# Running column sums on VectorE and loads on GpSimd's queue in a 2-D prefix-sum kernel

## The chip, the cores and the metric

The kernel runs on one core of a Trainium2 chip. The metric is the device time of one execution in microseconds (us). Every time below is the median of runs of one kernel, all fast. A ratio is the mean time of one kernel's fast runs over that of the other kernel's fast runs of the same rounds, so it is not quite the ratio of the medians quoted beside it. The "span" of a profile is some 2 us shorter than the device time, because it starts with the first instruction.

## The reference

Four matrices of 4224 x 4224 fp32 numbers (285.5 MB in all) are summed in two dimensions; the diagonal of the result is then summed once more.

```python
def reference(x):                      # x: (4, 4224, 4224) fp32
    ps = np.cumsum(np.cumsum(x, axis=1), axis=2)
    diag = np.diagonal(ps, axis1=1, axis2=2)
    return np.cumsum(diag, axis=1).astype(np.float32)
```

The diagonal element ps[i,i] is the sum of the upper left square. It grows from i-1 to i by the part of row i up to the diagonal and the part of column i above it. So the kernel needs, for every i, one row sum (to the left) and one column sum (above), and each element of the input is read once. What is left is a short chain of prefix sums.

## The kernel before

It walks through each image in 11 strips of 384 rows. A strip holds three rows in each of 128 partitions (P = 128, F = 3, GW = 384, NG = 11), and three strip buffers are in use. Strip g needs row sums over the columns left of the diagonal block, masked sums in the block itself, and column sums over all columns from the block on. This is the part that the change replaces (cuts marked):

```python
def load_rows(o, b, r0):
    nc.sync.dma_start(out=o, in_=x[b, r0 : r0 + GW, :].rearrange("(p f) w -> p f w", f=F))
# ...
def act_sum(acc, src):                              # row sum on ScalarE, output thrown away
    dump = dumpool.tile([P, 2688], BF16, name="dump")
    nc.scalar.activation(out=dump[:, :w], in_=src, func=ACT.Copy, accum_out=acc)
# ...
def add_up(strip, g, ws):
    k = row_of(g)
    hi = (g + 1) * GW
    mu = mup.tile([P, F, GW], FP32, name="mu")
    for q in range(F):
        act_sum(acc[:, k, q, 0:1], strip[:, q, :ws])             # ScalarE: 5/8 of the columns
    for q in range(F):
        block = strip[:, q, g * GW : hi]
        masked(mu[:, q, :], block, um3[:, q, :], ...)            # VectorE: diagonal block into mu
    for q in range(1, F):
        add_to(mu[:, 0, :], mu[:, q, :])
    columns(g, mu[:, 0, :], minus_sel)                           # TensorE: block's columns
    if hi < N:
        for q in range(1, F):
            add_to(strip[:, 0, hi:], strip[:, q, hi:])           # VectorE: 3 rows to 1
        for j in range(g + 1, NG):
            columns(j, strip[:, 0, j * GW : (j + 1) * GW])       # TensorE: all other columns
    for q in range(F):
        pair_sum(acc[:, k, q, 1:2], strip[:, q, ws:hi])          # VectorE: the other 3/8
```

At the end of the last image, strip 9 comes (strips count from 0), then the last 384 rows in pieces ("part_a", "part_b"). A chain of small steps closes the sum: row sums into PSUM, two scans (`c`), the rows' weights (`arows`, `fin_a`, `fin_b`, `fin_e`), and two small output transfers.

## Time and profile before

| | before |
|---|---|
| time, first runs | 677.53 us (676.79 to 678.20) |
| transfer queue busy | 98.2% of the span |
| VectorE, TensorE, ScalarE busy | 57%, 42%, 29% |
| last strip lands, end of span | 655.6 us, 675.7 us |

The table reads as follows: no engine is near its limit, and the input stream is nearly always at work. The trace holds sixteen completion records for each input transfer. I take them for one of each of the core's 16 DMA engines; the records carry no engine's name, so that a late record comes from the same engine every time is inferred from its steady delay. A transfer counts as landed when the sixteenth is there. I read these records one by one, and I call "lag" the distance from their median to the last of them.

### The profile page before, as it was taken

The numbers are of one execution on the slowest core, as the hardware profiler recorded it, in microseconds if no ns is written. First come the engines' busy times: TensorE is split into PE (matmuls) and PEld (weight loads), VectorE is DVE, ScalarE is ACT, GpSimd is POOL, SyncE is SP. The second block draws the span as 40 slices with busy tenths as digits, with TensorE's granted clock in tenths as the row PEclk, the third lists the DMA queues.
The fourth block names the chain that finished last, engine by engine and source line by source line (L and its number), as shares of the span: only waits on it lengthen the run. The fifth ranks groups of instructions, "written<-read, shape, count | busy, mean of one in ns | idle before, by whom it ended". The sixth has DMA issues, their size and how long they took to land.

```text
span 675.7 us, 2520 instructions
## 1 busy us (share of the span) xinstructions
PE 281.8 (42%) x576; PEld 70.3 (10%) x576; DVE 387.9 (57%) x738; ACT 198.0 (29%) x275; POOL 7.1 (1%) x30
## 2 busy tenths in 40 slices
PE   0366455521037644532105545543212555663224
PEld 0021111100002111100001111100000111110002
DVE  1678666443377766444347776544445777554556
ACT  0121322334412122233451112223453111222446
POOL 4000000000000000000000000000000000000000
PEclk9977766665557777755556877775655687766666
DMA  9999999999999999999999999999999999999993
GB/s 384 432 419 433 432 432 433 438 439 430 432 432 432 435 436 432 433 432 432 432 435 432 432 433 431 432 432 432 432 432 436 432 432 433 432 432 430 435 400 128
DMA packets 7938, 285.69 MB, mean 423 GB/s; under 512 B 840, under 2 KB 1396, under 8 KB 2164
## 3 DMA queue, kind: packets, MB, share of 16 engines
q1 hardware_dynamic: 7924, 285.55, 98.2%
q8 instruction: 4, 0.07, 0.0%
q14 instruction: 10, 0.08, 0.0%
HBM read 285.47 MB, written 0.07 MB: 423 GB/s over the span
## 4 chain that ended last, share of the span: by engine, by line
DMA 72%; DVE 13%; PE 11%; ACT 2%; issue 1%; SPq 0%; DVEq 0%; ACTq 0%
DMA strip<-in_x_dram 72%; PE d L207 10%; DVE strip L236 8%; DVE mu L239 2%; ACT dump L214 2%; DVE mu L236 2%; PE fin_b L207 0%; DVE pair L225 0%; DVE c L377 0%; PE fin_a L207 0%; SPq L69 0%; DVE c L239 0%; DVE pu L219 0%; DVE yl L416 0%; DVE r L219 0%
## 5 line engine op out<-in xcount | busy, mean ns | idle before, releaser
L214 ACT ACTIVATE dump<-strip 128x224 bf16<-128x224 f32 (+13 forms) x137 | 184.0, 1343 | 453.4 <-DMA strip<-in_x_dram 450.4
L207 PE MATMUL d<-strip,sel 128*33 128x384 f32 (+1 forms) x440 | 223.3, 677 | 130.6 <-DVE strip L236 130.6
L239 DVE SCALAR_TENSOR_TENSOR mu<-strip,um 128x384 f32<-128x384 f32 x129 | 65.2, 555 | 265.0 <-DMA strip<-in_x_dram 265.0
L236 DVE TENSOR_TENSOR strip<-strip 128x3840 f32<-128x3840 f32 (+9 forms) x80 | 188.4, 2355 | 1.4
L207 PE MATMUL d<-mu,minus_sel 128*33 128x384 f32 (+1 forms) x86 | 51.9, 698 | 249.6 <-DVE mu L236 249.6
L207 PEld LDWEIGHTS d<-strip,sel 128*33 128x33 f32 (+1 forms) x440 | 58.2, 140 | 301.6 <-DVE strip L236 170.5
L225 DVE SCALAR_TENSOR_TENSOR pair<-strip 128x80 bf16<-128x80 f32 (+12 forms) x138 | 81.7, 592 | 3.2
L236 DVE TENSOR_TENSOR mu<-mu 128x384 f32<-128x384 f32 x86 | 47.8, 556 | 1.5
L207 PEld LDWEIGHTS d<-mu,minus_sel 128*33 128x33 f32 (+1 forms) x86 | 7.2, 122 | 283.9 <-DVE mu L236 280.9
L214 ACT ACTIVATION_READ_ACCUMULATOR dump<-strip 128x1 f32 x137 | 25.5, 186 | 0.0
L225 DVE DVE_READ_ACCUMULATOR pair<-strip 128x1 f32 x138 | 11.3, 82 | 0.0
L239 DVE DVE_READ_ACCUMULATOR mu<-strip,um 128x1 f32 x129 | 10.7, 83 | 0.0
L214 ACT ACT_TABLE_LOAD x1 | 1.3, 1283 | 19.1 <-DMA strip<-in_x_dram 19.1
L207 PE MATMUL d<-ones_all,r 128*33 128x128 f32 (+1 forms) x12 | 2.3, 346 | 5.9 <-DVE r L219 5.9
L200 DVE TENSOR_SCALAR steps<-steps 128x128 int32<-128x128 int32 x1 | 0.5, 461 | 5.8 <-POOL steps L199 5.8
L207 PE MATMUL fin_a<-weights,arows 128*1 128x256 f32 (+1 forms) x4 | 1.4, 513 | 3.1 <-DVE arows L219 3.1
L207 PEld LDWEIGHTS d<-ones_all,r 128*33 128x33 f32 (+1 forms) x12 | 1.4, 132 | 8.7 <-issue 5.3
L219 DVE TENSOR_REDUCE r<-acc 128x99 f32<-128x297 f32 (+1 forms) x2 | 0.7, 360 | 2.6 <-ACT dump L214 2.6
L207 PE MATMUL fin_b<-weights,bsum 128*1 128x128 f32 (+2 forms) x12 | 2.1, 364 | 0.0
L377 DVE TENSOR_TENSOR_SCAN c<-ones_all,carry,c 33x384 f32<-33x384 f32 (+1 forms) x2 | 2.0, 1008 | 0.1
L102 DVE MEMSET um<- 128x1152 bf16 (+1 forms) x2 | 1.4, 698 | 1.1 <-PEq L465 1.1
L377 DVE TENSOR_TENSOR_SCAN c<-ones_all,carry,d 33x384 f32<-33x384 f32 (+1 forms) x2 | 2.0, 1002 | 0.1
(62 smaller groups left out, 23.8 us busy)
## 6 DMA issues: line engine op xcount, KB each, us to landing
strip<-in_x_dram SPq DMA_DIRECT2D x43, 6336.0 KB, 32.1
strip<-in_x_dram SPq DMA_DIRECT2D x1, 2304.0 KB
strip<-in_x_dram SPq DMA_DIRECT2D x1, 1536.0 KB
strip<-in_x_dram SPq DMA_DIRECT2D x3, 480.0 KB, 31.4
head<-in_x_dram SPq DMA_DIRECT2D x1, 576.0 KB
strip<-in_x_dram SPq DMA_DIRECT2D x1, 352.0 KB, 32.0
strip<-in_x_dram SPq DMA_DIRECT2D x1, 128.0 KB, 24.7
out_dram<-c SPq DMA_DIRECT2D x1, 49.5 KB
```

The lines of the kernel that those rows point to most:

```text
L102: nc.vector.memset(um, -1.0)
L200: nc.vector.tensor_single_scalar(out=steps, in_=steps, scalar=2, op=ALU.arith_shift_right)
L207: nc.tensor.matmul(o, lhsT=lhsT, rhs=rhs, start=start, stop=False, skip_group_check=True)
L214: nc.scalar.activation(out=dump[:, :w], in_=src, func=ACT.Copy, accum_out=acc)
L219: nc.vector.reduce_sum(out=acc, in_=src, axis=AX.X)
L225: nc.vector.scalar_tensor_tensor(out=pair[:, :w], in0=src[:, :w], scalar=1.0, in1=src[:, w:], op0=ALU.mult, op1=ALU.add, accum_out=acc,)
L236: nc.vector.tensor_add(out=o, in0=o, in1=i)
L239: nc.vector.scalar_tensor_tensor(out=o, in0=i, scalar=1.0, in1=m, op0=ALU.mult, op1=ALU.mult, accum_out=acc,)
L377: nc.vector.tensor_tensor_scan(out=c12[:, i, :], data0=ones_row[:rows], data1=src, initial=carry[:, i : i + 1], op0=ALU.mult, op1=ALU.add,)
```

## The change

The intent is to take work off TensorE: columns above the diagonal are added up on VectorE into one running row `u` per partition, and TensorE reads only 384 columns of it per strip. Masks are turned from -1 to 1. ScalarE now sums all the columns of a row and writes its unused output over the strip. The masked block is written over the strip too. All strips load by GpSimd's queue, and strip 9 of the last image comes in three transfers, one per row q ("thirds" below). Smaller edits are left out here, such as the place of the first sum of part_a, which now comes later. In diffs `...` and comment lines stand for code that is cut.

```diff
+    load = nc.gpsimd.dma_start
     def act_sum(acc, src):
-        dump = dumpool.tile([P, 2688], BF16, name="dump")
-        nc.scalar.activation(out=dump[:, :w], in_=src, func=ACT.Copy, accum_out=acc)
+        nc.scalar.activation(out=src, in_=src, func=ACT.Copy, accum_out=acc)
 ...
-        def add_up(strip, g, ws):            # shown above
+            for q in range(F):
+                act_sum(rsum[:, k, q : q + 1], strip[:, q, :hi])
+            block = strip[:, :, lo:hi]
+            nc.vector.tensor_mul(out=block, in0=block, in1=um3)
+            row_sums(rabove[:, k, :], block)
+            if g == 0:
+                nc.vector.tensor_add(out=u, in0=strip[:, 0, :], in1=strip[:, 1, :])
+                add_to(u, strip[:, 2, :])
+            else:
+                for q in range(F):
+                    add_to(u[:, lo:], strip[:, q, lo:])
+            columns(g, u_of(g))
 ...
+        if not whole:                        # strip 9 of the last image
+            columns(LG, head[:, 0, :])
+            for q in range(F):
+                load(out=strip[:, q, :], in_=rows_of(b, g)[:, q, :])
+            for q in range(F):
+                act_sum(rsum[:, k, q : q + 1], strip[:, q, :wa])
+                pair_sum(more[:, q : q + 1], strip[:, q, wa:hi])
+                masked(block, block, um3[:, q, :], rabove[:, k, q : q + 1])
+                add_to(u[:, lo:], strip[:, q, lo:])
+            for j in (g, LG):
+                columns(j, u_of(j))
```

## The prediction

> **What bounds the kernel now.** I read the page first: the head, the busy line of each engine, the slices, the queues.
>
> ```profile
> span 675.7 us, 2520 instructions
> ...
> PE 281.8 (42%) x576; PEld 70.3 (10%) x576; DVE 387.9 (57%) x738; ACT 198.0 (29%) x275; POOL 7.1 (1%) x30
> ...
> GB/s 384 432 419 433 432 432 433 438 439 430 432 432 432 435 436 432 433 432 432 432 435 432 432 433 431 432 432 432 432 432 436 432 432 433 432 432 430 435 400 128
> ...
> q1 hardware_dynamic: 7924, 285.55, 98.2%
> q8 instruction: 4, 0.07, 0.0%
> q14 instruction: 10, 0.08, 0.0%
> ```
>
> No compute engine is over 57% busy, while the one transfer queue is busy for 98.2% of the span and the rate stands at 432 to 433 GB/s in nearly every slice. 285.5 MB at 432 GB/s are 661 us. The kernel is a stream of input; compute matters only in the last 20 us, or if a buffer came free too late. So I then read how early transfers are asked for (the list of transfer issues), and the windows of the end:
>
> ```profile
> strip<-in_x_dram SPq DMA_DIRECT2D x43, 6336.0 KB, 32.1
> ```
>
> ```profile
> 500.00:640.00 140.00, 64.63 (x134) 14.14 (x134) 84.44 (x149) 36.00 (x54) 0.00 (x0) 0.67 1.00 433
> ...
> 660.00:665.00 5.00, 1.90 (x8) 0.48 (x6) 4.22 (x14) 4.91 (x7) 0.00 (x0) 0.84 0.79 310
> 665.00:670.00 5.00, 1.80 (x10) 0.62 (x11) 4.08 (x12) 4.81 (x13) 0.00 (x0) 0.50 0.07 27
> 670.00:676.00 6.00, 3.48 (x24) 2.38 (x22) 1.91 (x9) 0.47 (x2) 0.00 (x0) 0.50 0.00 0
> ```
>
> A strip (6.49 MB) takes 15.0 us to stream, and is issued 32.1 us before it lands: 45 - 32 = 13 us after the landing of the strip whose buffer it takes, with two others queued. There is slack of some 15 us. In the windows the last two columns are the DMA share and GB/s: from 665 on only 7% of the engines' capacity moves anything. I wanted to know why it is not zero, and why the last strip's compute starts at 655.68:
>
> ```profile
> 620.77 34.83 DMA strip<-in_x_dram
> 655.68 2.31 ACT dump L214 x2
> 658.00 2.31 ACT dump L214 x2
> 660.33 0.93 ACT dump L214
> ...
> 665.52 1.01 DVE c L377
> 666.56 1.00 DVE c L377
> 667.56 0.47 DVE pair L225 x2
> ```
>
> The trace keeps a completion record of each of the 16 DMA engines for each transfer. For the last strip 15 of them are at 649.10 to 651.04 us, and the sixteenth at 655.60. In the first strip the same gap is small (15 within 17.83 to 18.48, the last 19.06). So **one of the sixteen engines falls behind** during the run, and every strip waits for it. The packet records say why: its 50,688-byte packets, 1.875 us as a median, take 2.25 to 2.53 us at 55, 105, 145, 161, 254, 282, 403, 419, 421, 509, 564 and 615 us, and beside each of these there is a packet of an instruction queue (q14: 8,192 bytes; q8: 16,384 bytes). Instructions are fetched over that engine. In the strips' time 9 x 8,192 + 4 x 16,384 bytes went there, which at its 27.0 GB/s is 5.1 us; its lag against the median engine grew from 1.0 to 5.7 us, by 4.7. The end is the slow engine's landing (655.6) plus 20.1 us of chain; its very last piece lands at 669.96, and 5.8 us follow.
>
> **What the Trainium skill says.** (1) "DMA: Bandwidth & Descriptors", Where 436 GB/s comes from: the ports allow 435.2 GB/s. The trace agrees: 432 to 433. So no way of issuing can gain more than 0.7% of rate. (2) The same page, Latency and other measured facts, says that engines 7 and 15 are usually slower and puts this, as a guess, to the descriptor rings of the GpSimd (software) path, with no size. The trace before has no software queue, so it can't show it; its own straggler has the other cause above. (3) "SBUF — State Buffer", Who interferes with whom: VectorE in a 2-port mode locks GpSimd out and so starves its descriptor writing; `tensor_tensor` and `tensor_reduce` were not seen to. All large VectorE work after the change is of those two kinds; no run here shows it yet. (4) "VectorE: DVE Perf Modes", The TRN2 errata, gives (N+151)/0.96 ns for an fp32 add: 4.157 us for 3,840 columns. The trace agrees, 4155 ns:
>
> ```profile
> L236 DVE TENSOR_TENSOR strip<-strip 128x3840 f32<-128x3840 f32 x8 | 33.2, 4155 | 0.1
> ```
>
> **The change part by part.**
> TensorE: before, strip g sends 1 + (10-g) products of 384 columns, six on average; after, one. From 440 + 86 passes to about 90, at 0.68 to 0.70 us: 275 us of busy time become about 62, none of it on the path except in the tail.
> VectorE: the three masked blocks, two adds per block and pair sums (65.2 + 47.8 + 81.7 us) go, bar the tail. One multiply and one reduction of 1,152 elements come, 1.36 us by the add's formula and 1.35 (the head's reduction took 1347 ns). Adds into the running row: three per strip instead of two, over 384 more columns: three of 4.155 us for g=1 down to three of 0.94 for g=10, with two of 4.56 us for g=0. An image is 80 us of adds and 30 us of multiply and reduction, about 110; three of them, 100 for the nine first strips of the last and some 28 for the rest: **VectorE about 457 us**, from 388. Still under the 661.
> ScalarE: all columns up to hi instead of 5/8 of them. From 2400 columns in 2203 ns and 224 in 390: 0.203 us + 0.833 ns a column, + 0.19 for the accumulator. An image: 77 us; in all about 300, from 198.
> Buffer release: ScalarE now writes the strip in place, so VectorE must wait for all three sums, then works. g=1: 3 x 1.03 + 2.7 + 3 x 4.155 = 18.3 us after landing; g=5: 6.9 + 2.7 + 7.7 = 17.3; g=10: 11.7 + 2.7 + 2.8 = 17.2. Before it was 13. The other two strips last until 30 us after landing, so 12 us of slack remain less the GpSimd's time to write descriptors (a few us at most, my choice). VectorE's largest strip, 15.2 us, equals the stream's period only once per image, so no backlog builds. I take the stream to stay full.
> Queue: the bytes are the same, and packets should keep their 50,688 bytes. I choose the same rate, give or take 1%. The small head goes first by the old queue and should cover the new queue's start.
> Instructions: VectorE falls from 738 to about 285, TensorE and its loads from 1152 to about 260; GpSimd gains some 50. 2520 become about 1250. Half the fetches mean half the lag of the straggler: **-2.5 us**.
> Tail: the last strip comes in three pieces, so that at its landing L only one third is left: ScalarE 2.3 us, VectorE 2.5 (pair 0.9, mask 0.6, add 0.95), two products (1.5), the row sums into PSUM (0.9), the old sequence to the second scan (4.9), pair sums, row sum, closing products and output as before (8.2): L + 18.5 where it is L + 20.1 now. The last piece lands at L + 14.4 and needs at least some 4 us, also L + 18.4. Saving **1.6 us**, no more, as both limits meet there.
> Sum: 677.5 - 2.5 - 1.6 = 673.4, and I put 0.6 us on for a slower software queue: 674.0.
>
> **The rivals.**
> (A) The software queue is slower: ring reads, an engine that lags, or smaller packets. For: the skill's note on engines 7 and 15. Against: nothing in the trace. At 425 GB/s instead of 432 it is +11 us, 685; at 415, over 690.
> (B) Late buffers: descriptor writing is held up while VectorE runs (68% of the time), or the serial ScalarE-VectorE path eats the slack. It would show as slices below 430 GB/s. Against: 12 us of slack. It would be 680 to 700.
> (C) VectorE becomes the bound: 457 us against 661 speaks against it; only g=1 touches 15 us.
> (D) All hidden: the straggler stays (descriptors in place of instructions) and the tail is tied to the last landing: 676 to 678.
> (E) A gain over 2% (below 664.2): 661 us of stream plus 2 us of start alone come to 663, so the tail would have to vanish. Nearly excluded.
>
> **Range and chances.** My centre is 674.0. Without the straggler at all and with the tail's gain it would be about 670, a little better rate 667; (A) in a mild form gives 684. So 667 to 684 for 8 in 10. Over 691 needs (A) or (B) in earnest: 9%. Faster by over 2%: 2%. Within: 89%.
>
> **What would show it.** The queue's line must read software instead of hardware at the same MB, with 432 GB/s in the slices; TensorE below 90 us, VectorE 440 to 470, ScalarE near 300; fewer instruction packets, and the sixteenth landing of the last strips 2 to 4 us behind the rest rather than 5 to 6. From the last strip's landing to the end it should be 18 to 19 us. The prediction is wrong if slices drop below 425 GB/s, if packets are split, or if the gap between a landing and the next issue exceeds 27 us.

## The result, and the profile after

The changed kernel took 678.24 us (677.90 to 679.04, four runs) beside 677.75 us of the kernel before. The ratio is 1.0011, with a 95% interval of 0.9993 to 1.0028. A gain of 3.5 us was forecast; none came.

The first lines of the changed kernel's page, its slices and its queues:

```profile
span 676.2 us, 1095 instructions
...
PE 73.6 (11%) x138; PEld 12.8 (2%) x138; DVE 449.0 (66%) x277; ACT 276.3 (41%) x275; POOL 35.0 (5%) x81
...
GB/s 371 432 435 435 432 435 435 435 441 435 438 435 432 435 432 432 432 432 432 432 432 432 432 432 432 432 435 432 432 432 432 435 432 432 432 432 430 416 418 101
...
q0 software_dynamic: 7392, 284.89, 97.7%
q1 hardware_dynamic: 468, 0.66, 0.3%
q14 instruction: 7, 0.06, 0.0%
q8 instruction: 1, 0.02, 0.0%
```

The reader sees a large change that did what it was meant to do. TensorE fell from 281.8 to 73.6 us, instructions from 2520 to 1095, instruction packets from 14 to 8, and the stream kept its 432 GB/s on the new queue, but for 416 and 418 in the two slices from 625 to 659 us (the kernel before has 435 and 400 there, and e3_after_syncq below, on the old queue, 420 and 417). The stream even ended sooner. These are the completion records of both kernels (us; my reading of the traces):

```
                                 before: median  last   lag     after: median  last   lag
strip 8 of the last image             634.91  640.54   5.63         634.33  636.43   2.10
strip 9 (after: its last third)       649.90  655.60   5.69         649.49  651.61   2.12
last piece of all                     664.10  669.77   5.67         663.72  665.81   2.09
```

The last strip landed 4.0 us sooner, and so did the last piece. The end of the span did not move: from the landing of strip 9 to the end it was 20.1 us (675.7 - 655.6) and is now 24.6 us (676.2 - 651.6). The tail took back what the stream gave. The chain of waits of the changed kernel shows where (start, length, what):

```profile
608.94 27.49 DMA strip<-in_x_dram
...
636.54 5.00 ACT strip L211 x3
...
642.59 3.26 ACT strip L211 x3
...
645.88 1.37 DVE strip L297
...
649.92 1.37 DVE u L231
...
659.12 0.97 DVE u L231
...
660.14 3.64 PE d L205 x10
```

In the kernel before, the chain waits for strip 9. Here the last transfer in it is strip 8, which landed at 636.4 us. From then on it is work, 40 us of it: ScalarE until 645.8, VectorE until 660.1. VectorE's own timeline has the reason in its first line, in brackets (idle time before, and what ended it):

```profile
645.88 1.36 DVE L297 TENSOR_TENSOR strip<-strip,um 128x1152 f32<-128x1152 f32 x1 [7.97 <-ACT strip L211]
...
652.59 0.95 DVE L220 SCALAR_TENSOR_TENSOR pair<-strip 128x768 f32<-128x768 f32 x1
...
659.12 0.96 DVE L231 TENSOR_TENSOR u<-u,strip 128x768 f32<-128x768 f32 x1
```

VectorE stood idle for 8 us with strip 8 in memory, because ScalarE's three sums of 3,456 columns had to end first (9.2 us). It then did strip 8 (6.7 us) and the thirds of strip 9 one after another (7.4 us). Two of these thirds had landed long before. When the last third landed at 651.6, VectorE was 8.5 us away from the end of its work on it. In the kernel before, nothing wrote the strip that ScalarE was reading except past its columns, and VectorE started on strip 9 with the landing:

```profile
655.69 0.56 DVE L239 SCALAR_TENSOR_TENSOR mu<-strip,um 128x384 f32<-128x384 f32 x1 [8.08 <-DMA strip<-in_x_dram]
```

The same wait is there in nearly all strips. It is the longest line of VectorE in the list of waits (us in total, times, longest):

```profile
DVE strip L297 <- ACT strip L211: 203.4, 39, 10.4
```

These 203 us cost nothing in the earlier strips, since the stream does not wait for them: transfers were still issued 27.9 us (median) before they landed; e6_last_only below tests it.

### The profile page after: what moved, and what is told of

The parts are those of the page before. It is cut to its first block, busy times and chain, and to the rows that moved or that the text cites. A ratio compares the mean times of both kernels' runs of the same rounds, so it can differ in the third digit from the quotient of the medians.

```text
span 676.2 us, 1095 instructions
## 1 busy us (share of the span) xinstructions
PE 73.6 (11%) x138; PEld 12.8 (2%) x138; DVE 449.0 (66%) x277; ACT 276.3 (41%) x275; POOL 35.0 (5%) x81
## 4 chain that ended last, share of the span: by engine, by line
DMA 73%; ACT 10%; DVE 9%; issue 6%; PE 2%; ACTq 0%; DVEq 0%; POOLq 0%
DMA strip<-in_x_dram 73%; ACT strip L211 10%; DVE u L231 4%; DVE u L300 1%; DVE strip L297 1%; DVE above L214 1%; PE d L205 1%; DVE pair L220 1%; DVE c L379 0%; PE fin_b L205 0%; DVE strip L234 0%; PE fin_a L205 0%; DVE pu L214 0%; DVE c L234 0%; ACTq L211 0%
## 5 line engine op out<-in xcount | busy, mean ns | idle before, releaser
L211 ACT ACTIVATE strip<-strip 128x768 f32<-128x768 f32 (+11 forms) x137 | 270.5, 1975 | 389.0 <-DMA strip<-in_x_dram 374.7
L231 DVE TENSOR_TENSOR u<-u,strip 128x3840 f32<-128x3840 f32 (+10 forms) x121 | 299.1, 2472 | 2.9
L297 DVE TENSOR_TENSOR strip<-strip,um 128x1152 f32<-128x1152 f32 x42 | 57.0, 1357 | 203.4 <-ACT strip L211 203.4
L205 PE MATMUL d<-u,sel 128*33 128x384 f32 (+1 forms) x88 | 65.0, 844 | 593.9 <-DVE u L231 593.9
L214 DVE TENSOR_REDUCE above<-strip 128x3 f32<-128x1152 f32 x42 | 56.8, 1353 | 1.5
L292 POOL DMA_DIRECT2D strip<-in_x_dram x39 | 20.7, 530 | 574.6 <-DVE u L231 535.8
L211 ACT ACTIVATION_READ_ACCUMULATOR strip<-strip 128x1 f32 x137 | 25.5, 186 | 0.0
L205 PEld LDWEIGHTS d<-u,sel 128*33 128x33 f32 (+1 forms) x88 | 7.6, 134 | 648.7 <-DVE u L231 647.7
L300 DVE TENSOR_TENSOR u<-strip 128x4224 f32<-128x4224 f32 x4 | 18.2, 4549 | 0.0
L220 DVE SCALAR_TENSOR_TENSOR pair<-strip 128x384 f32<-128x384 f32 (+5 forms) x12 | 6.9, 577 | 0.2
L352 POOL DMA_DIRECT2D strip<-in_x_dram x5 | 2.7, 552 | 4.7 <-DMA strip<-in_x_dram 4.7
L316 POOL DMA_DIRECT2D strip<-in_x_dram x3 | 1.6, 528 | 14.2 <-issue 14.2
L341 POOL DMA_DIRECT2D strip<-in_x_dram x2 | 1.4, 709 | 13.2 <-issue 13.2
L86 POOL DMA_DIRECT2D strip<-in_x_dram x3 | 1.7, 594 | 0.8 <-POOLq L467 0.8
## 6 DMA issues: line engine op xcount, KB each, us to landing
strip<-in_x_dram POOLq DMA_DIRECT2D x42, 6336.0 KB, 27.9
```

The costliest lines, as they stand in the source:

```text
L86: load(out=t, in_=rows_of(0, i))
L205: nc.tensor.matmul(o, lhsT=lhsT, rhs=rhs, start=start, stop=False, skip_group_check=True)
L211: nc.scalar.activation(out=src, in_=src, func=ACT.Copy, accum_out=acc)
L214: nc.vector.reduce_sum(out=acc, in_=src, axis=AX.X)
L220: nc.vector.scalar_tensor_tensor(out=pair[:, :w], in0=src[:, :w], scalar=1.0, in1=src[:, w:], op0=ALU.mult, op1=ALU.add, accum_out=acc,)
L231: nc.vector.tensor_add(out=o, in0=o, in1=i)
```

## The experiments

**Theory.** Two things moved in opposite directions. (1) The DMA engine that lags is held up by instruction fetches; the change halved them, so landings came 4 us sooner. (2) In the last strips VectorE waits for ScalarE, since both write over the strip, and this costs the end some 5 us. **Rivals.** For the stream: the new queue removed the lag. For the tail: the closing products at a lower clock, or the last landing and what must follow it, set the end anyway.

All of the following runs were correct, with five rounds each beside the kernel before; e7_best has four timed runs and the changed kernel four. By a margin of 2% every one of them counts as "same", so the differences below are small ones, told by their intervals.

| run | median us | ratio to before | 95% interval | span us |
|---|---|---|---|---|
| changed kernel | 678.24 | 1.0011 | 0.9993 to 1.0028 | 676.2 |
| e1_scratch | 678.43 | 1.0008 | 0.9995 to 1.0022 | 676.8 |
| e2_apart | 673.17 | 0.9932 | 0.9920 to 0.9945 | 671.3 |
| e3_after_syncq | 678.14 | 1.0001 | 0.9988 to 1.0013 | 676.4 |
| e4_before_poolq | 677.65 | 0.9994 | 0.9981 to 1.0006 | 675.8 |
| e5_pad | 678.33 | 1.0010 | 0.9998 to 1.0023 | 676.6 |
| e6_last_only | 673.17 | 0.9927 | 0.9914 to 0.9941 | 671.5 |
| e7_best | 671.81 | 0.9914 | 0.9900 to 0.9927 | 669.8 |
| e8_pad_dve | 681.50 | 1.0061 | 1.0047 to 1.0075 | 679.3 |
| e9_pad_late | 681.15 | 1.0051 | 1.0037 to 1.0065 | 679.8 |

### The tail: who writes the strip

**e1_scratch** takes away one of the two writes:

```diff
-        nc.scalar.activation(out=src, in_=src, func=ACT.Copy, accum_out=acc)
+        dump = dumpool.tile([P, N], BF16, name="dump")
+        nc.scalar.activation(out=dump[:, : src.shape[-1]], in_=src, func=ACT.Copy, accum_out=acc)
```

> The changed kernel, with ScalarE's sums written to a bf16 scratch row instead of over the strip; the masking of the diagonal block still writes the strip in place. Theory (the tail's delay is that VectorE must wait for all three ScalarE sums of strip 8 of the last image): the masked block still overwrites columns that ScalarE has to read first, so this half of the undoing alone changes nothing: VectorE starts on that strip at about 645.9 us as in the changed kernel, end near 676 us, ratio to before 1.000. Rival (ScalarE's write into the strip is the whole of the wait): VectorE starts at the landing, 636.5 us, and the kernel ends near 670.5 us, ratio 0.990.

VectorE's first line on strip 8 in this run:

```profile
646.09 1.36 DVE L300 TENSOR_TENSOR strip<-strip,um 128x1152 f32<-128x1152 f32 x1 [7.96 <-ACT dump L212]
```

Nothing changed: the same idle time, the same engine named, and the same time of the kernel. ScalarE's write is not needed for the wait. VectorE's masked block overwrites columns that ScalarE has yet to read, and that alone keeps it waiting.

**e2_apart** takes the second write away as well:

```diff
-            nc.vector.tensor_mul(out=block, in0=block, in1=um3)
-            row_sums(rabove[:, k, :], block)
-            # adds over u[:, lo:] from the strip
+            nc.vector.tensor_mul(out=mu, in0=block, in1=um3)
+            row_sums(rabove[:, k, :], mu)
+            # adds over u[:, lo:hi] from mu, over u[:, hi:] from the strip
```

> As the run before, and the masked block goes to a tile of its own, so that nothing writes a strip any more and VectorE need not wait for ScalarE at all. Theory: VectorE starts on strip 8 of the last image at its landing (636.5 instead of 645.9 us), is through the last third of strip 9 at 654 instead of 660 us, and the span becomes 670 to 671 us, ratio to before 0.990 to 0.992. Rival (the tail is set by something else, the closing products at a lower clock or the last landing): VectorE starts early, but the end stays at 675 to 676 us, ratio 0.998 to 1.001.

VectorE in this run, on strip 8 and on the last add of strip 9:

```profile
637.38 1.36 DVE L301 TENSOR_TENSOR mu<-strip,um 128x1152 f32<-128x1152 f32 x1 [6.56 <-DMA strip<-in_x_dram]
...
654.14 0.96 DVE L234 TENSOR_TENSOR u<-u,strip 128x768 f32<-128x768 f32 x1
```

VectorE starts with the landing (this run's strip 8 landed at 637.35), and what ends its idle time is now the transfer. The last add is 5.0 us sooner, and the span is 4.9 us shorter, although strip 8 landed 0.9 us later than in the changed kernel. From the last third's landing (652.51) to the end it is now 18.8 us instead of 24.6. The time is 0.8% below the changed kernel's by the two ratios. The gain that the stream had made is now visible in the time.

The rival of the lower clock falls as well. In the changed kernel the granted clock was 0.50 while the four passes on `u` ran (660.14 to 662.87 us), and in e7_best below it was 1.00; the passes took 2.73 us in both. The profiled run of e1_scratch had a clock of 1.00 throughout and the changed kernel's time.

**e6_last_only** asks where the wait counts: the two tiles of their own are used in strip 8 of the last image alone.

```diff
+            apart = not whole and g == LG - 2
             for q in range(F):
-                act_sum(rsum[:, k, q : q + 1], strip[:, q, :hi])
+                act_sum(rsum[:, k, q : q + 1], strip[:, q, :hi], dump[:, :hi] if apart else None)
-            nc.vector.tensor_mul(out=block, in0=block, in1=um3)
+            masked_block = mu if apart else block
+            nc.vector.tensor_mul(out=masked_block, in0=block, in1=um3)
```

> The changed kernel with the separate tiles for ScalarE's output and the masked block in one strip alone, strip 8 of the last image. Theory (only the wait in that strip reaches the end; in the 41 others it lies under the transfers): at least as fast as with all strips apart, span 670 to 671.5 us, ratio 0.991 to 0.993. Rival (the waits in the earlier strips held transfers up too): half or less of the gain, ratio 0.996 or more.

One strip of 42 gives the whole gain: 0.9927 beside 0.9932. VectorE here goes from strip 7's work straight on to strip 8, 1.4 us after its landing (637.11), and in this run's list of waits it still waits for ScalarE in 38 strips:

```profile
638.50 1.35 DVE L307 TENSOR_TENSOR mu<-strip,um 128x1152 f32<-128x1152 f32 x1
...
DVE strip L307 <- ACT strip L211: 196.0, 38, 10.4
```

Taking these waits away as well (e2_apart) gained nothing more.

**e7_best** goes on from there. In strip 9 the running row is finished first, and its products start before the pair sums:

```diff
-                pair_sum(more[:, q : q + 1], strip[:, q, wa:hi])
-                masked(block, block, um3[:, q, :], rabove[:, k, q : q + 1])
-                add_to(u[:, lo:], strip[:, q, lo:])
-            for j in (g, LG):
-                columns(j, u_of(j))
+                masked(mu[:, q, :], block, um3[:, q, :], rabove[:, k, q : q + 1])
+                add_to(u[:, hi:], strip[:, q, hi:])
+                add_to(u[:, lo:hi], mu[:, q, :])
+                if q == F - 1:
+                    for j in (LG, g):
+                        columns(j, u_of(j))
+                pair_sum(more[:, q : q + 1], strip[:, q, wa:hi])
```

> As the run before, and in the last strip the running row is finished first (mask, add the columns above, add the block) and its products start before the pair sums. From the last strip's landing to the row sums in PSUM it should be 5 us where it was 6.4. Theory (the chain from that landing sets the end): about 1 us less than the run before, ratio 0.990 to 0.992. Rival (the last landing, near 666 us, and what must follow it set the end by now): less than 0.4 us better than the run before.

TensorE's timeline in this run has both groups of products:

```profile
652.51 2.73 PE L205 MATMUL d<-u,sel 128*11 128x384 f32 x4 [7.71 <-DVE u L233]
655.03 1.49 PE L205 MATMUL d<-ones_all,r 128*11 128x128 f32 x6
```

They start 1.1 us after the landing (651.39) and are done 5.1 us after it. The median is 1.4 us below e6_last_only, but the intervals of the two ratios overlap. The profiled runs differ in their lag too (2.1 us at the last piece here, 2.6 in e6_last_only), and the last third landed 0.9 us sooner. From that landing to the end it was 19.2 us in e6_last_only and is 18.4 here, so in these two runs 0.8 us is the reordering and the rest came with the stream. This version beats the kernel before by 0.9% and the changed kernel by 1.0%. From its last landing (665.93) to its end it is 3.9 us, of which the output transfers at the end are over 2, so little is left in the tail.

### The stream: what holds one engine back

**e3_after_syncq** is the changed kernel on the old queue, **e4_before_poolq** the kernel before on the new one:

```diff
 # e3_after_syncq
-    load = nc.gpsimd.dma_start
+    load = nc.sync.dma_start
 # e4_before_poolq, all loads but the head
-        nc.sync.dma_start(out=o, in_=x[b, r0 : r0 + GW, :] ...
+        nc.gpsimd.dma_start(out=o, in_=x[b, r0 : r0 + GW, :] ...
```

> The changed kernel with its strips loaded by the old queue of SyncE; nothing else. Theory (the slowest DMA engine lags because instructions are fetched over it, and there are fewer of them now): the lag of the sixteenth landing behind the median stays near 2 us at the end, the last landing near 666 us, time as in the changed kernel within 1 us, ratio 1.000 to 1.002. Rival (the queue removed the lag): the lag is 5 to 6 us as in the kernel before, last landing near 670 us, and the time 3 to 4 us longer, ratio 1.005 or more. A third (the queue costs something that hides a gain): ratio below 0.998.

> The kernel before with all its loads but the head issued by GpSimd's queue; its instructions otherwise as they were. Theory (instruction fetches make the lag): the lag stays 5 to 6 us, last landing near 670 us, ratio 0.999 to 1.003. Rival (the queue makes or removes the lag): the lag falls to about 2 us and the time by 3 to 4 us, ratio near 0.995.

Span and strip queue of e3_after_syncq, then of e4_before_poolq:

```profile
span 676.4 us, 1096 instructions
...
q1 hardware_dynamic: 8212, 285.55, 98.0%
```

```profile
span 675.8 us, 2520 instructions
...
q0 software_dynamic: 7104, 284.89, 97.8%
```

The four combinations of kernel and queue, lag at the last piece (us): before on the old queue 5.67, before on the new one 5.40, changed kernel on the new one 2.09, changed kernel on the old one 1.91. The lag goes with the instructions and not with the queue. Both ratios are within 0.1% of 1. The queue is neutral here, in lag, in rate and in time, as far as these runs can tell.

**e5_pad** was to test the fetches themselves, with results thrown away on an engine that has nothing to do:

```diff
             columns(g, u_of(g))
+            if whole or g < 7:
+                for _ in range(8):
+                    matmul(scr, sel[:, 0:1], sel[:, 0:2], start=True)
```

> The changed kernel with eight tiny products on the idle TensorE after each strip up to strip 6 of the last image (1,280 more instructions, results thrown away, no more data and no new wait). Theory (each 8,192 bytes of fetched instructions hold the slowest DMA engine up by 0.30 us, and strip 8's landing sets the end): ten more fetches, the lag of the sixteenth landing behind the median rises from 2.1 to about 5 us, the last landing from 665.8 to about 669 us, and the time by 3 us to about 681 us, ratio 1.004 to 1.006. Rival (instruction fetches do not slow the strips): lag near 2 us, ratio 1.001.

The expectation failed. Busy line and instruction queues of this run:

```profile
PE 92.8 (14%) x778; PEld 31.6 (5%) x778; DVE 449.0 (66%) x277; ACT 276.3 (41%) x275; POOL 35.2 (5%) x81
...
q8 instruction: 6, 0.10, 0.1%
q14 instruction: 7, 0.06, 0.0%
```

The added instructions were fetched: five more packets of 16,384 bytes on q8. Each 16,384-byte fetch still made one strip packet longer, by 0.46 to 0.55 us. But the last of the sixteen engines landed strip 8 at 636.38 us, as in the changed kernel (636.43), while the median moved from 634.33 to 635.59. So these fetches fell on other engines, which had room to be later (inferred from the records, which have no engine names). The prediction's picture, that all instructions come over one engine, is wrong.

So I looked at the steps of the slowest engine alone, from one strip to the next. They are 14.99 us, and in the kernel before they are 15.79 to 15.97 us at the strips that landed at 172, 293, 414, 520 and 626 us, with a smaller one of 15.26 at 66 us (and one of 15.17 at 111 us, after a 16,384-byte fetch at 103). Just ahead of these six, and six times only, an 8,192-byte instruction packet stands beside a strip packet stretched to 2.53 us: at 55, 161, 282, 403, 509 and 615 us. VectorE had 738 instructions; at 128 to a packet (64 bytes each: an estimate, from the 81,920 bytes more that e5_pad fetched for its 1,280 instructions) these are 5.8 packets. The changed kernel has 277 VectorE instructions (2.2 packets) and two such packets. Nobody arranged a third point, but e2_apart is one: it has 390 VectorE instructions (3.0 packets), three packets stretched to 2.53 us, and a lag of 2.96 us at strip 8, between 2.10 and 5.63. This pointed to VectorE's instructions alone.

**e8_pad_dve** puts the padding there:

```diff
             columns(g, u_of(g))
+            if whole or g < 7:
+                for _ in range(16):
+                    nc.vector.memset(pad, 0.0)
```

> The changed kernel with sixteen one-column memsets on VectorE after each strip up to strip 6 of the last image (640 more VectorE instructions of about 0.06 us, no more data and no new wait). The padding of TensorE added fetches but they fell on other DMA engines than the slowest and cost nothing. Theory, mended: VectorE's own instruction stream is fetched over the engine that lags, at 0.66 us of delay for each 8,192 bytes; five more fetches of it put the lag of the sixteenth landing behind the median from 2.1 to 5 or 5.5 us, the last landing from 665.8 to about 669 us and the time 3 us up, ratio 1.005 to 1.006. Rival (the lag is not made by VectorE's fetches but by what else the change did to the stream): lag near 2 us, ratio 1.000 to 1.002, or longer by VectorE's 40 us of work only if its backlog reaches the end.

The time rose by 0.5% over the changed kernel's, to 1.0061 by its ratio. The q14 packets rose by five, and strip 8 landed at 639.15 us instead of 636.43. Five steps grew to 15.90 to 16.02 us; two more, of 16.52 at 21 us and 15.30 at 141 us, are not among them, and no fetch stands before the first of these. The lag had reached 5.35 us at 503 us but was 4.22 at strip 8, under the 5 to 5.5 expected, because the other engines lost time as well. The slices show where, around 560 to 580 us:

```profile
GB/s 366 430 460 433 442 430 430 430 430 430 430 430 430 433 442 451 433 433 433 430 430 430 430 430 430 436 451 442 430 433 430 433 418 397 430 430 434 420 423 41
```

There VectorE's added work had let buffers come late (the transfer that landed at 579.4 us was issued 2.0 us before the median engine was through with the one before; in the changed kernel it was 8.4 us), so this run alone does not say which of the two cost the time.

**e9_pad_late** puts thirty memsets after strips 4 to 10 of the first three images, where VectorE has time to spare, and none in the last image:

```diff
-            if whole or g < 7:
-                for _ in range(16):
+            if whole and g >= 4:
+                for _ in range(30):
```

> As the padding of VectorE before, which also disturbed the stream at the start of the last image (slices down to 397 GB/s); now thirty memsets after each of the strips 4 to 10 of the first three images only, where VectorE has the least to do (630 more instructions, five more fetches), none in the last image. Theory: no slice below 425 GB/s before the tail, the lag of the sixteenth landing at strip 8 of the last image 2.1 + 5 x 0.66 = about 5 us, its landing near 639.5 us, ratio 1.004 to 1.006. Rival (the earlier padding cost time by VectorE's backlog, not by fetches): with the backlog gone the lag may grow but the time is that of the changed kernel, ratio 1.000 to 1.002.

VectorE's instructions are 907 here, by the busy line (the slices below it):

```profile
PE 74.6 (11%) x138; PEld 12.9 (2%) x138; DVE 485.1 (71%) x907; ACT 276.3 (41%) x275; POOL 35.0 (5%) x81
...
GB/s 372 444 444 444 429 427 432 429 427 429 429 438 447 436 436 429 438 427 429 429 429 433 435 444 444 430 432 430 429 429 433 432 415 429 429 432 430 420 412 15
```

The lag at strip 8 was 5.67 us and its landing at 639.42, 3.0 us later than in the changed kernel; the ratio was 1.0051. Seven steps of the slowest engine were longer, and each goes with one of seven q14 fetches that I take for VectorE's (six steps of 15.90 to 16.07 us, one of 15.61); three further q14 fetches, near 145, 253 and 432 us, stand at about these times in the changed kernel too. The wish for a clean stream was not quite met: one slice still fell to 415 GB/s, near 550 us. In that stretch the slowest engine, which sets the landings, lost 0.45 us in one step and, later, 0.2 in another, so late buffers can have made some 0.7 of the 3.0 us. Five more fetches at about 0.95 us each, less what some 33 ordinary steps gained (14.94 instead of 14.99 us), come to about 3 us (an estimate). What makes the ordinary steps a little shorter in the padded runs I did not find out.

## Why the prediction was right or wrong

**Right: what bounds the kernel.** The stream stayed at 432 GB/s and VectorE and TensorE moved as forecast: TensorE 73.6 us plus its loads (under 90), VectorE 449 us (440 to 470), ScalarE 276 us where near 300 was given (its two lines on the page add up to 296; they overlap). Rivals (A), (B) and (C) did not come: no slower queue (e3, e4), no late buffers (issues 27.9 us ahead of landing; 45 - 28 = 17 us after the old strip's landing, as the part on buffer release has it), no bound on VectorE. Two slices did fall below the 425 GB/s that the prediction gave as a sign of being wrong, but at the end only, and on the old queue as well (e3). Rival (D) comes nearest to the result with its 676 to 678 us, for a wrong reason: it had the straggler stay, and its lag fell to 2.1 us.

**Right with another mechanism and a low size: the straggler.** The direction was right, -2.5 us forecast and -4.0 us measured in the last strip's landing. Wrong was the picture behind the size, that all fetches go over one engine at 0.30 us for 8,192 bytes. Only VectorE's pile up on one engine here, and each costs the slowest engine 0.8 to 1.0 us (e5, e8, e9). Four packets less at some 0.95 us are 3.8 us (an estimate), near the 4.0 measured. That the forecast had the right sign is partly luck: it would have been the same for a change that spared only TensorE's instructions, and e5 shows that 1,280 instructions more for TensorE cost the landing nothing. Six packets were as good an account of the lag as thirteen shorter ones, which is why the sum had looked right.

**The step that failed: the tail.** The prediction said: "the last strip comes in three pieces, so that at its landing L only one third is left: ... VectorE 2.5". At L, VectorE had 8.5 us of work left, not 2.5: it was still in strip 8 and had all three thirds of strip 9 before it. The ScalarE-VectorE waits that I had worked out for three strips under buffer release ("VectorE must wait for all three sums") were used there for the question whether buffers come free in time, and were not carried on to the end, where the same wait is on the path. The rest of that sum was mis-sized only a little: the products took 2.73 us where 1.5 was put, and the way to the second scan 4.2 where 4.9 was put; the row sums (0.9) and the closing part (8.2) were as forecast. The terms add up to 2.5 + 1.5 + 0.9 + 4.9 + 8.2 = 18.0, where the prediction writes 18.5; 6.0 more in VectorE and 0.6 in the rest are the 24.6 us measured. e2 and e6 show this to be the cause: with the wait gone, from all strips or from one, the kernel took 673.17 us, and from L to the end it was 18.8 and 19.2 us. That is within 1 us of the 674.0 forecast, though this agreement has its own luck: in e2 the stream gave 3.1 us where 2.5 was put, the tail 1.3 where 1.6 was put, and the 0.6 us added for a slower queue did not come.

**Slips that changed nothing.** For g=10 the prediction puts three adds of 0.94 us; by its own formula that is g=9, and g=10 has three of 0.56 (its sum of 80 us an image is right). The last piece landed at 669.77 us, not 669.96; the latter is the last record of an output transfer issued at 655.6. The fetched bytes at 27.0 GB/s are 5.2 us, not 5.1.

**The net.** -4.0 us in the stream and +4.5 us in the tail make +0.5 us of span (675.7 to 676.2), and +0.5 us of median time.

## What to carry to other kernels

A wait that costs nothing in forty strips can be on the path in the last one: work out the last buffers' chain by itself, engine by engine, with the backlog that each engine has when the last data arrive. Writing in place saves memory, but it makes the engines that share a tile take turns, and a read on one engine is enough for that. In a kernel bound by its input, look at the single completion records of a transfer: here the latest set every landing, and fewer instructions on VectorE brought it forward by 4 us, while more of them on TensorE did not move it.

## What the Trainium skill lacked or had wrong

- "Runtime: NRT & Kernel Launch", Instruction fetch mechanics, says that crossing a block of instructions is mostly hidden. What it costs the engine that fetches was not looked at here; for a full input stream it was not hidden. VectorE's fetches came in packets of 8,192 bytes (six packets for 738 instructions, two for 277), and each held up one DMA engine by 0.8 to 1.0 us a time once that engine was the slowest. The page gives blocks of 16 KiB; q8 had these (16,384 bytes), q14 had 8,192.
- "DMA: Bandwidth & Descriptors", Latency and other measured facts, puts slow DMA engines, as a guess, to the software path's descriptor rings. One engine (its number is not in the records) lagged on either path, by 5.67 us (hardware) and 5.40 us (software) with 738 VectorE instructions, and by 1.91 and 2.09 us with 277. The queue made no difference that these runs could see.
